# Biased attention on one core: how the last batches of output are closed and who issues their stores

## The chip, the cores and the metric

The kernel runs on one core of a Trainium2 chip. Its engines work side by side: TensorE (PE, with its weight loads shown apart as PEld), VectorE (DVE), ScalarE (ACT), GpSimd (POOL) and SyncE (SP). ScalarE, SyncE and GpSimd can also issue DMAs. In the profile "SPq" and "ACTq" are the instruction queues of SyncE and ScalarE when they issue a DMA or wait. The metric is the device time of one execution in microseconds (us); lower is better. A run's time is a little longer than its profile's span, which goes from the first to the last instruction.

## What is computed

Attention over 4 x 8 = 32 heads, 1024 positions, 64 columns per head, with one bias matrix shared by all heads:

```python
scores = scale * np.matmul(q, k.transpose(0, 1, 3, 2)) + bias
attn = np.exp(scores - scores_max) / (np.sum(np.exp(scores - scores_max), axis=-1, keepdims=True) + 1e-8)
return np.matmul(attn, v)
```

The kernel leaves out the subtraction of the maximum. It gives V a column of ones, so that the sum of the exponentials comes out of the same product as the result, and divides at the end.

## The kernel before

**Slots.** The work is cut into 256 slots. A slot is one head and one of eight chunks of 128 queries; all 1024 keys are done at once. A slot lives in one of three PSUM places (pl0, pl1, pl2), each 128x1024 f32. A slot goes through three steps:

- `fill` (L246, matmuls at L244): TensorE adds q times k for the slot to what its place holds from the slot before. A fill is 8 matmuls, and it must wait until the place's earlier contents have been read.
- `exp` (L253, L258): ScalarE takes the exponential of the place into an SBUF tile `E`. For 19 slots listed in `PLAN`, the last of them slot 243, VectorE does this instead, by a polynomial in six steps (L275, L280, L284, L287, L290, L295), into a tile `de`.
- `av` (L303, matmuls at L312): TensorE multiplies the exponentials by V, 8 matmuls, into 65 columns of a PSUM bank `po`.

**Batches.** Up to seven slots share one `po` bank and make a batch. A batch is closed by `close` (L680), which queues `evac` (L315) on VectorE: a reciprocal of the sums (`rs`, L320) and a multiplication (L322) that writes the finished columns to SBUF. A batch of more than one slot goes to a tile `ob`, of which there are two buffers (L60); a batch of one goes to a tile of its own, `olast` (L74). There are two `po` banks. They are taken in turn by the batches, so that a new batch waits until the batch before the last has been evacuated.

**Stores.** `evac` makes one store to DRAM of each run of neighbouring chunks of one head. A run of one chunk gives 128 rows of 256 bytes (64 columns, 32 KB), of two 64 KB, and of three 96 KB.

**Rounds.** The slots come in rounds. At the end of the kernel a round is three slots of one head, one for each place, with the chunks 0, 1 and 2: slots 247, 248, 249 are a round, then 250 to 252, and 253 to 255. Slot 246 is the last one of the round before. Slot 243 is taken out of the row of its round, since its `de` tile is finished much later.

**Order.** Nothing is reordered on the chip: a planner in the kernel goes through the work with estimated costs and writes out the order in which the instructions of each engine stand. A batch is closed when it has seven slots, or six with no finished `de` tile at hand, or when 255 or 256 slots are done (L638). In `close`, `last` is true for the batches that end with slot 255's neighbour or slot 255: ScalarE issues their stores, all of them, and SyncE those of all other batches (L688). Stores marked `last` stand behind ScalarE's last exponential in its order.

In the order of before, the eleven slots that come last in `av` make three batches:

| batch | slots | stores, issued by |
|---|---|---|
| six slots | 246, 247, 248, 249, 250, 251 | 32 KB, 96 KB, 64 KB by SyncE |
| four slots | 252, 243 (`de`), 253, 254 | 32 KB, 32 KB, 64 KB by ScalarE |
| one slot | 255 | 32 KB by ScalarE |

When all is done, SyncE waits for every store and then all engines go through a closing barrier (shown as L835).

Of the kernel before, what the change touches and what calls it, by code (L numbers as in the profile page):

```python
# [16 lines left out]
def kernel(  # L17
# [13 lines left out]
    nc = tc.nc  # L31
# [59 lines left out]
    round_of = []  # L91
# [19 lines left out]
    NS = len(slots)  # L111
# [191 lines left out]
    def av(group, b, tag):  # L303

        if b not in bank:
            bank[b] = [ps_x.tile([P, 7, D1], F32, tag=tag, name="po"), []]
        po, units = bank[b]
        j = len(units)
        units += group
        for kc in range(NCH):  # L310
            for i, s in enumerate(group):
                nc.tensor.matmul(po[:, j + i, :], etile[s][:, kc, :], vall[:, slots[s][2] % VR, kc, :],  # L312
                                 start=j + i + kc == 0, stop=kc == NCH - 1, skip_group_check=True)

    def evac(b):  # L315

        po, units = bank[b]
        n = len(units)
        rs = small.tile([P, 7, 1], F32, name="rs")
        nc.vector.reciprocal(rs[:, :n, :], po[:, :n, D:D1])  # L320
        ob = olast if n == 1 else op.tile([P, 7, D], F32, name="ob")
        nc.vector.tensor_tensor(ob[:, :n, :], po[:, :n, :D], rs[:, :n, :].to_broadcast([P, n, D]), op=ALU.mult)  # L322
        stores = []

        j = 0
        while j < n:
            x, c, h, start = slots[units[j]]
            i = j + 1
            while i < n and slots[units[i]][1:3] == (c + i - j, h):
                i += 1  # L330
            stores.append((of[:, h, c:c + i - j, :], ob[:, j:i, :]))
            j = i
        return stores

    with tc.manual_schedule():
# [4 lines left out]
        for i in range(2):  # L340
            nc.sync.dma_start(out=k0f[:, :, i * half:(i + 1) * half].rearrange("p t c d -> p t (c d)"),
                              in_=kf[0][:, :, i * half * D:(i + 1) * half * D])
# [52 lines left out]
        L_PE, L_ACT, L_DVE = 205, 210, 140  # L395
# [10 lines left out]
        av_done = {}  # L406
# [21 lines left out]
        dav = []  # L428
# [9 lines left out]
        sp_q, t_sp = [], T0  # L438
# [43 lines left out]
        def next_v(t):  # L482

            while loads_v and not any(x[2] // 2 == loads_v[0] - VR // 2 and y not in av_done for y, x in enumerate(slots)):
                if loads_v[0] - VL not in v_at:
                    break
                p = loads_v.pop(0)
                vland_at[p] = issue(t, 1600, LATE + (p > 12), load_v, p) + 2000
                move_v(p)
# [86 lines left out]
        def pe_cands():  # L576

            out = []
            for x in range(3):
                if not queue[x] or queue[x][0] > next_fill + WINDOW:  # L580
                    continue
                s = queue[x][0]
                r = fill_ready(s)
                if r is not None and (before[s] is None or before[s] in used):
                    cost = FILL + BIAS * bool(slots[s][3] and s > 1)

                    def do(t, s=s, x=x, cost=cost):
                        nonlocal next_fill
                        fill(s)
                        filled[s] = t + cost + L_PE  # L590
                        queue[x].pop(0)
                        next_fill = min([y[0] for y in queue.values() if y], default=NS)
                        if s in PLAN:
                            dslots.add(s)
                            avq.remove(s)
                            start_d(s)
                        else:
                            acts.append(s)
                    out.append((max(t_pe, r), cost, do, 0, s))
# [3 lines left out]
            if avq:  # L603
                group = [s for s in avq[:1] if round_of[s] == round_of[avq[0]]]
                have = [s for s in group if s in e_at]
                lag = len([s for s in avq[:NE] if s in e_at])
                if len(have) < len(group):
                    group = have if lag >= 7 and have[:1] == avq[:1] else []
                if avq[0] >= NS - 3:
                    group = [s for s in avq[:1] if s in e_at]  # L610
# [4 lines left out]
            if todo:  # L615
                r, group = min(todo)
                b = len(closed)
                if b_tag:
                    tag = b_tag[0]
                    group = group[:7 - len(bank[b][1])]  # L620
                else:
                    f, tag = min((x_free[y], y) for y in x_free)
                    r = max(r, f)
                cost = AVG * len(group) if len(group) > 1 else AV
                if r < 1e11:
                    def do(t, group=group, b=b, tag=tag, cost=cost):
                        b_tag[:] = [tag]
                        x_free[tag] = 1e12
                        av(group, b, tag)
                        for s in group:  # L630
                            if s in dslots:
                                dav.pop(0)
                            else:
                                avq.remove(s)
                            av_done[s] = t + cost
                        next_v(t)
                        n = len(bank[b][1])
                        if n == 7 or n == 6 and not (dav and dav[0][0] < t + cost + 600) or len(av_done) in (NS - 1, NS):  # L638
                            closed.append(b)
                            b_tag.clear()  # L640
                            close(b, tag, t + cost + L_PE)
                    out.append((max(t_pe, r), cost, do, 1, 0))
            if pieces:
                pr, which, c0, n = pieces[0]
                need = need_at[pr, which, c0]
                ring = pr + linked(pr) - RING
                lag = len([s for s in avq[:NE] if s in e_at])
                if ((pr, which, c0) in raw_at and next_fill >= need - AHEAD and (ring < 0 or last_slot[ring] < next_fill)
                        and (lag < 4 or need - next_fill < 8)):
                    f, tag = min((x_free[y], y) for y in x_free)  # L650
                    r = max(f, raw_at[pr, which, c0])
                    cost = n * TR + SWITCH * (pr < EARLY or which not in BESIDE)
                    urgent = need - next_fill < 12
                    if r < 1e11:
                        def do(t, pr=pr, which=which, c0=c0, n=n, tag=tag, cost=cost):
                            x_free[tag] = 1e12
                            pieces.pop(0)
                            px = transposes(pr, which, c0, n, tag)
                            if pr < EARLY and which == 0 and c0 == 0:
                                freed(pr, t)  # L660

                            def run(t2):
                                copy_out(pr, which, c0, n, px)
                                done = t2 + 60 * n + (180 if which else 300)
                                x_free[tag] = done + L_DVE
                                if which:
                                    ready["ko", pr] = done + L_DVE
                                else:
                                    ready["qo", pr, c0] = done + L_DVE
                                doubles(pr, which, c0, n, done, urgent)  # L670
                            dve_q.append((t + cost + L_PE, 0 if urgent else 2, 60 * n + (180 if which else 300), run))
                        out.append((max(t_pe, r), cost, do, 2 if next_fill < need - 12 else 0.5, 0))
# [7 lines left out]
        def close(b, tag, t):  # L680
            units = bank[b][1]
            cost = 230 + 120 + 67 * len(units)
            last = len(av_done) >= NS - 1

            def run(t2):
                for to, of_ in evac(b):

                    w = nc.scalar if last else nc.sync  # L688
                    sp_q.append((t2 + cost + L_DVE, lambda t3, to=to, of_=of_: w.dma_start(out=to, in_=of_), last))  # L689
                x_free[tag] = t2 + cost + L_DVE  # L690
            dve_q.append((t, 1, cost, run))

# [76 lines left out]
        while next_fill < NS or next_act < len(acts) or avq or dav or dve_q or sp_q:  # L769
# [15 lines left out]
            stores = [x for x in sp_q if len(x) == 2 or not x[2] or next_act == len(acts)]  # L785
# [6 lines left out]
            t, who = min(c)  # L792
# [47 lines left out]
```

## Time and profile before

| | us |
|---|---|
| three runs | 234.78, 236.41, 235.97 (median 235.97) |
| the profiled execution | 235.12 |
| its span | 233.4 |
| around the span | 1.72 |

The granted TensorE clock of the core is 0.996. ScalarE, TensorE and VectorE are all over 80% busy, and the page's strip of 40 slices shows them so from the fifth slice on:

```profile
## 2 busy tenths in 40 slices
PE   7899998899999999999999999999999999999992
...
DVE  3576777599988998889989789899999899999991
ACT  3699999899999999999999999999999999999992
POOL 8754540276563636304254010000000000000000
```

Each digit is the busy share of 5.8 us, in tenths. Only the last slice is nearly empty: the kernel runs full until some 4 us before its end. GpSimd has been done since the middle.

### The profile page before, as it was taken

The page shows a single profiled execution, that of the slowest core. Times are in us where ns is not written, and L with a number is a line of the kernel's source. Part 1 is how long each engine was busy: PE and PEld are TensorE (multiplying, and loading weights), DVE is VectorE, ACT ScalarE, POOL GpSimd, SP SyncE. Part 2 cuts the span into 40 slices and gives each one's busy share as a digit, 9 for nine tenths or more (in the row PEclk, how much of TensorE's full clock was granted, in tenths as well). Part 3 has the DMA queues.
Part 4 walks back from the last instruction along what each step waited for, and adds up shares of the span by engine and source line. Part 5 has one row for each costly group of instructions (what it writes and reads, how often), then busy time and mean ns, then how long its engine had stood idle before and what let it go on. Part 6 is the DMA issues. An engine that isn't in the chain of part 4 may idle for free.

```text
span 233.4 us, 10661 instructions
## 1 busy us (share of the span) xinstructions
PE 222.4 (95%) x4671; PEld 209.6 (90%) x4671; DVE 197.7 (85%) x290; ACT 221.6 (95%) x242; POOL 61.7 (26%) x99
## 2 busy tenths in 40 slices
PE   7899998899999999999999999999999999999992
PEld 2779997899999999998999999999998999999991
DVE  3576777599988998889989789899999899999991
ACT  3699999899999999999999999999999999999992
POOL 8754540276563636304254010000000000000000
PEclk9999999999999999999999999999999999999998
DMA  6999999899997999989899764111111112112112
GB/s 207 207 206 218 221 226 215 180 112 142 171 173 119 139 188 149 181 188 138 148 234 232 162 108 128 37 37 42 42 40 43 45 42 75 49 31 80 44 37 62
DMA packets 55645, 29.75 MB, mean 127 GB/s; under 512 B 31728, under 2 KB 51952, under 8 KB 55600
## 3 DMA queue, kind: packets, MB, share of 16 engines
q0 software_dynamic: 30336, 14.06, 48.5%
q1 hardware_dynamic: 24544, 14.33, 22.0%
q10 hardware_dynamic: 720, 0.69, 1.1%
q8 instruction: 36, 0.59, 1.1%
q14 instruction: 9, 0.07, 0.1%
HBM read 29.36 MB, written 8.39 MB: 162 GB/s over the span
## 4 chain that ended last, share of the span: by engine, by line
PE 44%; ACT 29%; issue 14%; DVE 5%; DMA 4%; SPq 2%; POOL 1%; DVEq 0%; ACTq 0%; POOLq 0%
ACT E L258 29%; PE pl L244 25%; PE po L312 12%; PE px L191 4%; DMA braw<-in_bias_dram 2%; PE pl L241 2%; SPq L689 2%; DMA out_dram<-ob 1%; DVE ob L322 1%; PE px L187 1%; DVE df L280 1%; DVE dy L275 1%; DVE dt L290 0%; DVE df L287 0%; DVE rs L320 0%
## 5 line engine op out<-in xcount | busy, mean ns | idle before, releaser
L258 ACT ACTIVATE E<-pl 128x1024 bf16<-128x1024 f32 (+1 forms) x238 | 218.4, 1119 | 3.4 <-PE pl L244 3.0
L312 PE MATMUL po<-vall,E 128*128 128x65 bf16 x1896 | 91.9, 194 | 1.7 <-ACT E L258 0.9
L312 PEld LDWEIGHTS <-E 128*128 128x128 bf16 x1896 | 77.4, 98 | 2.8 <-ACT E L258 1.2
L244 PE MATMUL pl<-qo,ko 128*128 128x128 bf16 x1024 | 76.9, 219 | 1.1 <-ACT E L258 0.6
L244 PEld LDWEIGHTS <-ko 128*128 128x128 bf16 x1160 | 69.4, 98 | 3.9 <-issue 0.9
L244 PE MATMUL pl<-qe,ke 128*128 128x128 bf16 x888 | 66.2, 219 | 2.1 <-issue 0.7
L244 PEld LDWEIGHTS <-ke 128*128 128x128 bf16 x888 | 53.4, 98 | 4.9 <-issue 1.3
L275 DVE TENSOR_SCALAR dy<-pl 128x1024 int32<-128x1024 f32 x19 | 23.2, 1221 | 4.4 <-PE pl L244 3.6
L322 DVE TENSOR_TENSOR ob<-po,rs 128x448 f32<-128x448 f32 (+2 forms) x39 | 23.2, 594 | 2.3 <-DVE rs L320 0.4
L284 DVE SCALAR_TENSOR_TENSOR dt<-df 128x1024 f32<-128x1024 f32 x19 | 23.2, 1220 | 0.3
L295 DVE SCALAR_TENSOR_TENSOR de<-dy,dt 128x1024 uint16<-128x1024 int32 x19 | 23.2, 1219 | 0.2
L287 DVE SCALAR_TENSOR_TENSOR df<-dt,df 128x1024 f32<-128x1024 f32 x19 | 23.1, 1220 | 0.1
L290 DVE SCALAR_TENSOR_TENSOR dt<-df,dt 128x1024 f32<-128x1024 f32 x19 | 23.1, 1219 | 0.1
L138 POOL DMA_DIRECT2D q<-in_q_dram x18 | 16.4, 911 | 7.0 <-DVE rs L320 5.4
L165 POOL DMA_DIRECT2D v<-in_v_dram x16 | 11.3, 705 | 20.9 <-DVE rs L320 9.9
L199 DVE COPY ko<-px 128x1024 bf16<-128x1024 bf16 (+1 forms) x16 | 10.8, 672 | 6.6 <-PE px L191 6.2
L201 DVE TENSOR_SCALAR qo<-px,sgn 128x1024 bf16<-128x1024 bf16 (+2 forms) x18 | 12.4, 686 | 4.2 <-PE px L191 2.6
L320 DVE RECIPROCAL rs<-po 128x7 f32<-128x7 f32 (+3 forms) x40 | 7.9, 197 | 7.2 <-PE po L312 7.0
L280 DVE TENSOR_SCALAR df<-dy 128x1024 f32<-128x1024 uint16 x19 | 13.3, 700 | 0.1
L241 PE MATMUL pl<-ident,braw 128*128 128x128 bf16 x136 | 11.6, 229 | 0.4 <-DMA braw<-in_bias_dram 0.3
L145 POOL DMA_DIRECT2D k<-in_k_dram x15 | 10.7, 713 | 2.2 <-DMA k<-in_k_dram 1.2
L241 PEld LDWEIGHTS <-braw 128*128 128x128 bf16 x136 | 9.9, 149 | 0.7 <-DMA braw<-in_bias_dram 0.5
(54 smaller groups left out, 119.9 us busy)
## 6 DMA issues: line engine op xcount, KB each, us to landing
v<-in_v_dram POOLq DMA_DIRECT2D x16, 256.0 KB, 6.1
k<-in_k_dram POOLq DMA_DIRECT2D x15, 256.0 KB, 6.3
out_dram<-ob SPq DMA_DIRECT2D x34, 96.0 KB, 3.6
ke<-ko SPq DMA_DIRECT2D x22, 128.0 KB, 4.7
out_dram<-ob SPq DMA_DIRECT2D x41, 64.0 KB, 2.3
q<-in_q_dram POOLq DMA_DIRECT2D x18, 128.0 KB, 4.9
qe<-q SPq DMA_DIRECT2D x17, 128.0 KB, 4.4
out_dram<-ob SPq DMA_DIRECT2D x67, 32.0 KB, 2.8
```

Of the source, the lines that this page charges most:

```text
L138: nc.gpsimd.dma_start(out=t[:, :, y, :], in_=(qf, kf)[x][pr][:, y].rearrange("p (c d) -> p c d", d=D))
L241: nc.tensor.matmul(to, braw[:, c, :].rearrange("p (kp kc) -> p kc kp", kc=NCH)[:, kc, :], ident8[:], start=i == 0, stop=False, skip_group_ ...
L244: nc.tensor.matmul(to, kk[:, kc, :], qq[:, c, :], start=False, stop=True, skip_group_check=True)
L258: nc.scalar.activation(e[:, i:i + n].rearrange("p b x -> p (b x)"), places[slots[s][0]][:, i:i + n].rearrange("p b x -> p (b x)"), ACTF.Ex ...
L275: w.tensor_scalar(t["y"][:], places[slots[s][0]].rearrange("p b x -> p (b x)"), scale * LOG2E * 65536.0, 127.0 * 65536.0, op0=ALU.mult, op ...
L280: w.tensor_scalar(t["f"][:], t["lo"], G / 65536.0, None, op0=ALU.mult)
L284: w.scalar_tensor_tensor(t["t"][:], t["f"][:], -G, t["f"][:], op0=ALU.add, op1=ALU.mult)
L287: w.scalar_tensor_tensor(t["f"][:], t["t"][:], Q, t["f"][:], op0=ALU.mult, op1=ALU.add)
L290: w.scalar_tensor_tensor(t["t"][:], t["f"][:], V, t["t"][:], op0=ALU.add, op1=ALU.mult)
L295: w.scalar_tensor_tensor(etile[s].bitcast(U16).rearrange("p c q -> p (c q)"), t["y"][:], 1.0 / 512.0, t["t"][:], op0=ALU.mult, op1=ALU.add)
L312: nc.tensor.matmul(po[:, j + i, :], etile[s][:, kc, :], vall[:, slots[s][2] % VR, kc, :], start=j + i + kc == 0, stop=kc == NCH - 1, skip_ ...
L322: nc.vector.tensor_tensor(ob[:, :n, :], po[:, :n, :D], rs[:, :n, :].to_broadcast([P, n, D]), op=ALU.mult)
```

## The change

```diff
                         n = len(bank[b][1])
-                        if n == 7 or n == 6 and not (dav and dav[0][0] < t + cost + 600) or len(av_done) in (NS - 1, NS):
+
+                        z = group[-1]
+                        if (n == 7 or n == 6 and not (dav and dav[0][0] < t + cost + 600) or len(av_done) == NS
+                                or z >= NS - 2 or z >= NS - 10 and round_of[z] != round_of[z + 1]):
                             closed.append(b)
@@ in close
             def run(t2):
-                for to, of_ in evac(b):
-
-                    w = nc.scalar if last else nc.sync
-                    sp_q.append((t2 + cost + L_DVE, lambda t3, to=to, of_=of_: w.dma_start(out=to, in_=of_), last))
+                stores = evac(b)
+                for i, (to, of_) in enumerate(stores):
+
+                    end = last and i == len(stores) - 1
+                    w = nc.scalar if end else nc.sync
+                    sp_q.append((t2 + cost + L_DVE, lambda t3, to=to, of_=of_, w=w: w.dma_start(out=to, in_=of_), end))
```

The first part closes a batch after slot 246 and from there on wherever a round ends, and after slots 254 and 255. The second part leaves to ScalarE only the last store of each of the last two batches and gives the others to SyncE. The eleven slots now make five batches:

| batch | slots | stores, issued by |
|---|---|---|
| one slot (`olast`) | 246 | 32 KB by SyncE |
| three slots | 247, 248, 249 | 96 KB by SyncE |
| three slots | 250, 251, 252 | 96 KB by SyncE |
| three slots | 253, 243 (`de`), 254 | 32 KB (253) and 32 KB (243) by SyncE, 32 KB (254) by ScalarE |
| one slot (`olast`) | 255 | 32 KB by ScalarE |

Slot 243 now stands between 253 and 254 in its batch, so that the chunks of 253 and 254 are no longer neighbours and go out in two stores.

On the engines: TensorE has the same matmuls, in another order over the last 240 rows of its order. VectorE has two reciprocals and two multiplications more (five pairs for the three of before), and the first two extra pairs stand ahead of steps L287 and L295 of slot 243. ScalarE issues two stores where it issued four; SyncE issues five where it issued three. All instructions ahead of that, some 222 us of the profiled execution, are the same on every engine.

## The prediction

> **What bounds the kernel now.** I read the page first, for the engine that is full; then the stretch from 222 us on in order of time for ScalarE, VectorE and TensorE, since nothing ahead of it changes; then the DMA view of the last microseconds and SyncE's waits, for what ends the run.
>
> The page's totals, and ScalarE from 222 us (start, length, engine, line, operation, count):
>
> ```profile
> PE 222.4 (95%) x4671; PEld 209.6 (90%) x4671; DVE 197.7 (85%) x290; ACT 221.6 (95%) x242; POOL 61.7 (26%) x99
> ```
> ```profile
> 221.62 7.57 ACT L258 ACTIVATE E<-pl 128x1024 bf16<-128x1024 f32 x8
> 229.47 1.31 ACTq L689 DMA_DIRECT2D out_dram<-ob  x3
> 230.88 0.39 ACTq L689 DMA_DIRECT2D out_dram<-olast  x1
> ```
>
> ScalarE runs eight exponentials without a gap. One lasts about 1.15 us and the next starts 0.92 us after it (7.57 less 1.15, over 7), so they end at 222.75, 223.67, 224.60, 225.52, 226.43, 227.35, 228.27 and 229.19. Then it issues three stores back to back until 230.78, and only then that of `olast`. VectorE in the same stretch:
>
> ```profile
> 222.52 0.19 DVE L320 RECIPROCAL rs<-po 128x6 f32<-128x6 f32 x1
> 222.74 0.56 DVE L322 TENSOR_TENSOR ob<-po,rs 128x384 f32<-128x384 f32 x1
> 223.22 1.21 DVE L287 SCALAR_TENSOR_TENSOR df<-dt,df 128x1024 f32<-128x1024 f32 x1
> 224.47 1.23 DVE L290 SCALAR_TENSOR_TENSOR dt<-df,dt 128x1024 f32<-128x1024 f32 x1
> 225.73 1.23 DVE L295 SCALAR_TENSOR_TENSOR de<-dy,dt 128x1024 uint16<-128x1024 int32 x1
> 226.87 0.19 DVE L320 RECIPROCAL rs<-po 128x6 f32<-128x6 f32 x1
> 227.09 0.56 DVE L322 TENSOR_TENSOR ob<-po,rs 128x384 f32<-128x384 f32 x1
> 228.80 0.18 DVE L320 RECIPROCAL rs<-po 128x4 f32<-128x4 f32 x1 [1.15 <-PE po L312]
> 229.01 0.42 DVE L322 TENSOR_TENSOR ob<-po,rs 128x256 f32<-128x256 f32 x1
> 229.71 0.17 DVE L320 RECIPROCAL rs<-po 128x1 f32<-128x1 f32 x1 [0.28 <-PE po L312]
> 229.91 0.23 DVE L322 TENSOR_TENSOR olast<-po,rs 128x64 f32<-128x64 f32 x1
> ```
>
> `olast` is complete at 230.14, and its store starts at 230.88: 0.74 us in which the last result waits for ScalarE's queue. `ob` ended at 229.43 and its store began at 229.47, so a store needs only 0.04 us after its data. Then the landing, from the DMA view of 228 us on (KB each, us from issue to landing), the row of the page for large stores, and SyncE's last wait:
>
> ```profile
> out_dram<-ob SPq DMA_DIRECT2D x1, 96.0 KB, 1.7
> out_dram<-olast ACTq DMA_DIRECT2D x1, 32.0 KB, 1.5
> ```
> ```profile
> out_dram<-ob SPq DMA_DIRECT2D x34, 96.0 KB, 3.6
> ```
> ```profile
> SPq L835 <- DMA out_dram<-olast: 0.4, 1, 0.4
> ```
>
> The store of `olast` lands at 230.88 + 1.5 = 232.38, it is the last thing waited for, and 1.0 us of closing barrier brings the span to 233.4. So the path of the end is: last exponential 229.19, its product (229.24 to 229.67), the `olast` pair (to 230.14), 0.74 us of queue, 1.5 us of landing, 1.0 us of barrier.
>
> **ScalarE's two stores fewer.** The three stores ahead of `olast` (0.35 + 0.44 + 0.44, with gaps 1.31 us) become one of 0.35 us. It can start when `ob` of the batch of 253, 243, 254 is written. That batch's last product is slot 254's, as before, so its reciprocal starts at 228.80 again; the multiplication has 192 columns, which by the rows of 64 (0.23) and 256 columns (0.42) takes 0.36 us: 229.01 to 229.37. ScalarE's store then runs from 229.41 to 229.76, and ScalarE is free when `olast` is complete at 230.14. The store of `olast` starts at 230.18 where it was 230.88: **minus 0.70 us**.
>
> **SyncE's two stores more.** They start at 229.41 and about 229.76 (0.35 us, then 0.43 us). SyncE was free from 228.95 on in before; here the 96 KB store of slots 250 to 252 comes just ahead, from 228.42 to about 228.85. The second of the two lands at 229.76 + 1.55 = 231.31, ahead of `olast` at 230.18 + 1.5 = 231.68. Cost nothing; if an issue took 1.18 us, as one of SyncE's at 223.7 did, the second would start at 230.59 and land at 232.14, and 0.46 of the 0.70 would be lost.
>
> **Four small stores close together.** Before, one of them had 512-byte rows; now all four have 256-byte rows, since 243 splits 253 from 254. This strip is 231.2 to 232.2 in 40 slices, each digit the busy share of the 16 DMA engines:
>
> ```profile
> DMA  0000559899986421000000034899774210000000
> ```
>
> The first burst is the 64 KB store, 0.35 us; the second is `olast`, 32 KB, 0.30 us, 0.87 us after its issue. The two 32 KB bursts ahead of them took 0.28 us. Stacked one after the other from 229.41 + 0.87 = 230.28, four bursts of 0.28 end at 231.40; `olast` alone would end at 230.18 + 0.87 + 0.28 = 231.33. So contention costs nothing to 0.07 us; I take 0.06, as two are issued at the same moment. The Trainium skill ("DMA: Bandwidth & Descriptors", Specifications) says that a transfer needs at least 512 B for line rate, since below this the DMA engine reads, modifies and writes; this speaks against the split. The trace agrees that half the bytes are hardly cheaper. By the rule taken whole, 32 KB in short rows would be as dear as 64 KB in long ones, which leaves an estimated gain of 0.35; rival 1 works this out from rows.
>
> **VectorE's two pairs more.** A pair of 64 columns takes 0.43 us (229.71 to 230.14), one of 192 columns 0.57. Before L287 comes the pair of slot 246: L287 moves from 223.22 to 223.63, L290 ends at 226.11. Then the pair of 247 to 249, whose last product (slot 249) is there by 225.5: to 226.64. L295 then ends at 227.87, where it ended at 226.96. Its `de` is wanted by slot 243's product, which now stands behind that of 253 (exponential done 227.35, product started by 227.68), so TensorE waits for `de` until 227.9 and is done issuing it by 228.19, ahead of slot 254 at 228.33. The pair of 250 to 252 fills 227.87 to 228.42, ahead of 228.80. Cost nothing, under this cover: `de` may be 0.14 us later before slot 254's product moves, and another 0.34 before its pair runs into the `olast` pair at 229.71. Beyond 0.48 us every bit shows.
>
> **TensorE's order.** Two bank changes more, each with a wait for an evacuation. Slot 247 waits for the bank that VectorE frees at 223.30 (the pair at 222.52 above). Ahead of it stands a fill that was behind it, released by the exponential that ended at 222.75:
>
> ```profile
> 222.42 0.68 PE L312 MATMUL po<-vall,E 128*128 128x65 bf16 x16
> 222.93 0.61 PE L244 MATMUL pl<-qe,ke 128*128 128x128 bf16 x8
> 224.66 0.61 PE L244 MATMUL pl<-qe,ke 128*128 128x128 bf16 x8 [0.31 <-ACT E L258]
> 229.24 0.43 PE L312 MATMUL po<-vall,E 128*128 128x65 bf16 x8 [0.48 <-ACT E L258]
> ```
>
> With it the fill runs from about 222.8 to 223.25 and the wait is 0.1 us. The later banks are free at 223.65, 226.64 and 228.42, ahead of their use at 225.4, 227.4 and 229.24. TensorE must be ready for the fill at 224.66, since the exponential at 225.3 follows it directly; from 223.33 it has 0.26 + 0.45 + 0.26 us of issuing for that (eight `av` matmuls take half of the first row's 0.52, eight fills 0.45), so 0.36 us are left. Cost nothing; past that, ScalarE stalls by the excess.
>
> **Sum.** -0.70 + 0.06 = -0.64 us: the span 233.4 becomes 232.76, the profiled time 235.12 becomes 234.48. That execution lies 0.85 below the median; the median, 235.97, becomes 235.33. What is late next is the landing and the barrier, which stay.
>
> **Rivals.**
> 1. *A part of the gain* (0 to 0.5 us): the SyncE issue of 1.18 us, the stacked bursts, or `de` late. If VectorE's extra 0.41 + 0.50 us ahead of L295 cost twice that, 0.43 of it passes the cover and the gain is 0.21: 235.8. If a 32 KB burst among others takes the 0.35 us of the 64 KB one, the four end at 231.68 and the gain is 0.35: 235.6; I give this 0.05 of the rival's chance, as both lone 32 KB bursts ahead took 0.28. For the long issue: one took 1.18. Against: the other eleven after 214 us took 0.33 to 0.43.
> 2. *The second `ob` buffer decides, and it gets slower.* The `ob` of 253, 243, 254 reuses the buffer of slots 247 to 249, whose 96 KB store is issued only at 226.68. If that lands later than 229.0 (2.3 us after its issue) the pair waits; past 229.34 (2.7 us) `olast` stands behind it on VectorE; past 3.4 us the whole gain is gone. With the page's 3.6 us it lands at 230.28, the pair ends at 230.64, `olast` at 231.07 and its store starts at 231.11: 0.23 later than before, 236.2. For: 3.6 is the median of all 34. Against: that was with loads on the DMA engines; the row of the last microseconds has 1.7.
> 3. *More than forecast*: the fill at 222.93 moves ahead by 0.13 us, and if ScalarE turned out to follow TensorE there, that would come on top: gain 0.8, 235.2. ScalarE has no gap, so little speaks for it.
>
> That the change does not reach the chip's order is no case here: the order of stores and pairs is written out.
>
> **Chances and range.** Forecast 0.70, rival 1 0.17, rival 2 0.08, rival 3 0.05. All cases lie within 1% (2.36 us, about what a measurement can tell from no change), so faster or slower by over 1% could come only from the scatter of runs, 234.78 to 236.41 in before: 0.03 each. The range takes the lowest of those less 0.70, 234.1, up to the highest with nothing gained, 236.4.
>
> **What would show it.** Right: `olast`'s store issued within 0.1 us of its multiplication, the last exponential still ending near 229.2, no gap on ScalarE from 222 us on, L295 about 0.9 us later with TensorE waiting for `de` and not for slot 254's place, the span near 232.8. Wrong: a gap on ScalarE at 225.3, VectorE waiting for a store ahead of the 192-column multiplication at 229.0, or SyncE's last wait on a store of `ob` instead of `olast`.

## The result and the profile after

| | before | after |
|---|---|---|
| median, first comparison | 235.42 us (8 runs) | 234.21 us (8 runs) |
| ratio, 95% interval | | 0.9948 [0.9922, 0.9973] |
| profiled execution | 235.12 us | 234.37 us |
| its span | 233.4 us | 232.6 us |
| last exponential ends | 229.19 us | 229.16 us |
| from there to the end of the span | 4.2 us | 3.4 us |

The kernel became about half a percent faster in this comparison, and 0.4% faster in two later ones (below). The two profiled executions differ by 0.75 us and their spans by 0.80, of which 0.77 lies behind the last exponential. This stretch, from the end of the last exponential to the end of the span, is called the tail below. The pages of the profile round the span to 0.1 us; the traces end at 233.355 and 232.557, so the tails are 4.17 and 3.40 us. The tails below are reckoned from such ends, while the expectations were written with rounded spans (3.44 for after). The tail can be compared between profiles, since it leaves out the first 229 us, whose length changes from run to run by more than the gain: in the traces of this case the last exponential ends anywhere from 228.54 to 229.48 us.

ScalarE after, in order of time (start, length, engine, line, operation, count):

```profile
217.97 11.19 ACT L258 ACTIVATE E<-pl 128x1024 bf16<-128x1024 f32 x12
229.38 0.36 ACTq L694 DMA_DIRECT2D out_dram<-ob  x1
230.15 0.34 ACTq L694 DMA_DIRECT2D out_dram<-olast  x1
```

The twelve exponentials are one unbroken stretch. One store stands ahead of `olast`'s where three stood, and ScalarE is idle from 229.74 until the last result is there. VectorE after:

```profile
223.19 0.16 DVE L320 RECIPROCAL rs<-po 128x1 f32<-128x1 f32 x1
223.38 0.22 DVE L322 TENSOR_TENSOR olast<-po,rs 128x64 f32<-128x64 f32 x1
223.53 1.21 DVE L287 SCALAR_TENSOR_TENSOR df<-dt,df 128x1024 f32<-128x1024 f32 x1
224.77 1.23 DVE L290 SCALAR_TENSOR_TENSOR dt<-df,dt 128x1024 f32<-128x1024 f32 x1
225.91 0.17 DVE L320 RECIPROCAL rs<-po 128x3 f32<-128x3 f32 x1
226.12 0.36 DVE L322 TENSOR_TENSOR ob<-po,rs 128x192 f32<-128x192 f32 x1
226.40 1.22 DVE L295 SCALAR_TENSOR_TENSOR de<-dy,dt 128x1024 uint16<-128x1024 int32 x1
...
228.99 0.36 DVE L322 TENSOR_TENSOR ob<-po,rs 128x192 f32<-128x192 f32 x1
229.69 0.17 DVE L320 RECIPROCAL rs<-po 128x1 f32<-128x1 f32 x1 [0.34 <-PE po L312]
229.89 0.23 DVE L322 TENSOR_TENSOR olast<-po,rs 128x64 f32<-128x64 f32 x1
```

The last multiplication ends at 230.12 and its store starts at 230.15. Before, the two were 0.74 us apart. The extra pairs stand ahead of L287 and L295; L295 ends at 227.62. TensorE after, some of its rows:

```profile
222.80 0.61 PE L244 MATMUL pl<-qe,ke 128*128 128x128 bf16 x8
223.33 0.43 PE L312 MATMUL po<-vall,E 128*128 128x65 bf16 x8
224.63 0.61 PE L244 MATMUL pl<-qe,ke 128*128 128x128 bf16 x8
227.67 0.43 PE L312 MATMUL po<-vall,de 128*128 128x65 bf16 x8
229.22 0.43 PE L312 MATMUL po<-vall,E 128*128 128x65 bf16 x8 [0.48 <-ACT E L258]
```

The fill that was at 222.93 stands ahead of the product at 223.33, the fill that ScalarE follows is at 224.63 where it was at 224.66, and slot 243's product (`de`) starts at 227.67, 0.05 us after its tile is complete and well ahead of slot 254's, which starts at 228.30. TensorE hardly waits for the tile: slot 253's product keeps it issuing until about 227.65. SyncE's last two stores (the row spans both), the landings of the last stores, and SyncE's last waits:

```profile
229.37 0.81 SPq L694 DMA_DIRECT2D out_dram<-ob  x2
```
```profile
out_dram<-ob SPq DMA_DIRECT2D x2, 32.0 KB, 1.5
out_dram<-ob ACTq DMA_DIRECT2D x1, 32.0 KB, 1.7
out_dram<-olast ACTq DMA_DIRECT2D x1, 32.0 KB, 1.5
```
```profile
SPq L840 <- DMA out_dram<-ob: 0.7, 2, 0.5
SPq L840 <- DMA out_dram<-olast: 0.3, 1, 0.3
```

`olast` is still the last store to land, 1.5 us after its issue. By the trace, the 0.77 us of the tail are 0.71 us by which its store starts earlier, 0.05 by which it lands sooner after that (1.51 to 1.45), and 0.01 behind the landing. The issue itself became 0.05 us shorter, too: it took 0.39 us directly behind three other stores and takes 0.34 on an idle queue.

### The profile page after: what moved, and what is told of

It is laid out like the page before. It is cut to its first block, busy times and chain, and to the rows that moved or that the text cites. A ratio compares the mean times of both kernels' runs of the same rounds, so it can differ in the third digit from the quotient of the medians.

```text
span 232.6 us, 10671 instructions
## 1 busy us (share of the span) xinstructions
PE 223.1 (96%) x4671; PEld 209.8 (90%) x4671; DVE 197.4 (85%) x294; ACT 221.6 (95%) x242; POOL 61.6 (27%) x99
## 4 chain that ended last, share of the span: by engine, by line
PE 42%; ACT 30%; issue 14%; DMA 5%; DVE 4%; POOL 3%; SPq 2%; DVEq 0%; ACTq 0%; POOLq 0%
ACT E L258 30%; PE pl L244 24%; PE po L312 12%; DMA q<-in_q_dram 4%; PE px L191 4%; SPq L694 2%; PE pl L241 2%; DVE ob L322 1%; DMA out_dram<-ob 1%; DVE dy L275 1%; POOL k L145 1%; DVE df L280 1%; POOL braw L160 1%; DVE dt L290 0%; DVE de L295 0%
## 5 line engine op out<-in xcount | busy, mean ns | idle before, releaser
L295 DVE SCALAR_TENSOR_TENSOR de<-dy,dt 128x1024 uint16<-128x1024 int32 x19 | 23.1, 1218 | 0.1
L287 DVE SCALAR_TENSOR_TENSOR df<-dt,df 128x1024 f32<-128x1024 f32 x19 | 23.1, 1218 | 0.1
L468 POOL COPY tick<-q 1x1 bf16<-1x1 bf16 x9 | 3.3, 365 | 28.4 <-DMA q<-in_q_dram 28.4
```

The source lines that it names most:

```text
L287: w.scalar_tensor_tensor(t["f"][:], t["t"][:], Q, t["f"][:], op0=ALU.mult, op1=ALU.add)
L295: w.scalar_tensor_tensor(etile[s].bitcast(U16).rearrange("p c q -> p (c q)"), t["y"][:], 1.0 / 512.0, t["t"][:], op0=ALU.mult, op1=ALU.add)
```

## The experiments

The theory was: the gain is the time that the last result waited in ScalarE's queue, so it belongs to the second part of the change. The rivals: it belongs to the closing by rounds; or a part of the measured 1.2 us comes from somewhere else. In the diffs, three dots stand for further lines.

**The second part alone.** The kernel before, with the new `close` and the old condition for closing.

```diff
-                for to, of_ in evac(b):
-                    w = nc.scalar if last else nc.sync
+                stores = evac(b)
+                for i, (to, of_) in enumerate(stores):
+                    end = last and i == len(stores) - 1
+                    w = nc.scalar if end else nc.sync
...
```

> Only the second part of the change: the batches close as before, ScalarE issues the last store of each of the last two. Measured by the tail, from the end of the last exponential to the end of the span: 4.2 us in before, 3.44 in after. Theory (the whole gain is the wait of the last result behind ScalarE's stores): ScalarE issues one 64 KB store at 229.47 and the olast store at 230.18; tail 3.4 to 3.5, the time within 0.3 us of after. Rival (closing by rounds carries the gain): tail near 4.2, time as before.

Median 234.57 us, ratio 0.9973 [0.9947, 0.9998]. The last exponential ends at 229.16, the span at 232.6: a tail of 3.42 us, for 3.40 in after. ScalarE in this kernel:

```profile
223.40 5.76 ACT L258 ACTIVATE E<-pl 128x1024 bf16<-128x1024 f32 x6
229.44 0.37 ACTq L691 DMA_DIRECT2D out_dram<-ob  x1
230.14 0.34 ACTq L691 DMA_DIRECT2D out_dram<-olast  x1
```

`olast`'s store starts 0.98 us after the last exponential, as in after (0.99), with the old three batches. So the second part alone gives 0.75 of the 0.77 us. The time was expected within 0.3 us of after, and this was missed: measured beside it, after has 234.18 (below), 0.39 less. The twelve runs of this kernel spread from 233.33 to 235.65, and the profiles leave no place for 0.39 us: from the start of the eighth last exponential to the end of the last one it is 7.56 us in both kernels, and ahead of that their instructions are the same. So it is taken for scatter.

**The first part alone.** The changed kernel with the old `close`.

```diff
-                stores = evac(b)
-                for i, (to, of_) in enumerate(stores):
-                    end = last and i == len(stores) - 1
-                    w = nc.scalar if end else nc.sync
...
+                for to, of_ in evac(b):
+                    w = nc.scalar if last else nc.sync
...
```

> Only the first part of the change: batches close with their rounds, and ScalarE issues all four stores of the last two batches. Theory: three stores of 32 KB from 229.41 to about 230.68 stand ahead of olast, whose store starts at about 230.78 instead of 230.88; tail 4.1, gain 0.1 us at most. Rival (closing by rounds carries the gain): tail 3.5 to 3.7.

Median 234.80 us, ratio 0.9987 [0.9967, 1.0007]; the tail is 4.09 us (229.46 to 233.54), where 4.1 was expected. ScalarE:

```profile
223.70 5.76 ACT L258 ACTIVATE E<-pl 128x1024 bf16<-128x1024 f32 x6
229.67 1.31 ACTq L692 DMA_DIRECT2D out_dram<-ob  x3
231.08 0.39 ACTq L692 DMA_DIRECT2D out_dram<-olast  x1
```

Here `olast`'s store starts 1.62 us after the last exponential, against 1.69 in before: 0.07 us, because the multiplication has 192 columns for 256 (0.36 for 0.42 us). This is all that the closing by rounds brings by itself, and beside the second part it brings next to nothing (a tail of 3.40 us for 3.42).

**Another way out of the queue.** The kernel before, with nothing changed but the engine that issues the store of `olast`.

```diff
-                    w = nc.scalar if last else nc.sync
...
+                    end = last and len(stores) > 1
+                    w = nc.scalar if end else nc.sync
...
```

> Before, with one store moved: ScalarE keeps the three stores of the batch of four, SyncE issues that of olast. Theory: SyncE is free, olast is issued at 230.18 and lands at 231.7, but ScalarE's third store, 64 KB, issued at 230.34, lands at 231.94 and now ends the run: tail 3.75, gain 0.45 us, and SyncE's last long wait is on ob. Rival (SyncE starts a store later than ScalarE does, or the order of SyncE's waits matters): tail 4.0 or more.

The tail is 3.77 us (228.84 to 232.61), where 3.75 was expected; the median is 234.44 us, and the ratio 0.9990 [0.9964, 1.0016] doesn't tell this from no change. ScalarE's three stores and SyncE's one:

```profile
229.12 1.31 ACTq L690 DMA_DIRECT2D out_dram<-ob  x3
```
```profile
229.82 0.33 SPq L690 DMA_DIRECT2D out_dram<-olast  x1
```

`olast` starts 0.98 us after the last exponential from SyncE too and lands in 1.5 us, so it doesn't matter here which of the two engines issues it, only that nothing is queued ahead. ScalarE's third store, the 64 KB one, is now the last: issued at 229.99, it lands 2.80 us after the last exponential, where `olast` lands 2.44 us after it in after. The Trainium skill ("DMA: Bandwidth & Descriptors", Issuing engines are not separate DMA queues) says that issuing from several engines saves only the sequencer's time to start a DMA, usually small beside the DMA itself. The traces agree: a landing still takes 1.5 to 1.7 us, an issue 0.33 to 0.44. But three issues in a row ahead of the last result are 1.31 us, and at the end of a program nothing hides them.

**Is the rest scatter?** The tails differ by 0.77 us; the first medians by 1.21. The changed kernel was run again, and a third time beside the halves (below).

> The changed kernel once more, beside new runs of before. The tails of the two profiles differ by 0.77 us, the medians by 1.2. If the rest is scatter of the runs of before (which lie in two clusters, 234.6 to 234.9 and 235.9 to 236.4): the difference here is nearer to 0.77, or the runs of the other kernels of this call, whose first 222 us are the same, show the upper cluster too. If it belongs to the change: the difference is 1.2 again and no run of this kernel is above 235.

> After, in the same call as the halves, so that both share the runs of before. Expected ratio about 0.9967 (tail shorter by 0.77 us of 235); the median within 0.3 us of the halves.

| | before | after | ratio |
|---|---|---|---|
| first | 235.42 (8 runs) | 234.21 (8) | 0.9948 [0.9922, 0.9973] |
| second | 234.97 (35) | 234.18 (12) | 0.9964 [0.9943, 0.9984] |
| third | 234.93 (23) | 234.19 (12) | 0.9957 [0.9939, 0.9976] |

After gives 234.2 each time; it is before that moves. With 35 and 23 runs of before the medians differ by 0.79 and 0.74, which fits the tail. The two clusters of the first eight runs of before are not there in the 35, which fill the gap between them, and the other kernels measured beside them go up to 235.5 and beyond too. The tail itself repeats: it is 3.40, 3.39 and 3.40 us in the three profiles of after (of before there is one). All three intervals hold 0.9967 (0.77 of 235), though all three ratios lie below it. So a further tenth of a percent can't be excluded, but the profiles show no place for it: the last eight exponentials take 7.56 to 7.57 us in before and in all three of after, and ahead of them every engine has the same instructions in the same order.

**The output buffer.** The three batches of three slots share one buffer, in a tile that is dead by then.

```diff
-        ob = olast if n == 1 else op.tile([P, 7, D], F32, name="ob")
+        ob = olast if n == 1 else qz[0].bitcast(F32).rearrange("p c x -> p (c x)")[:, :3 * D].rearrange("p (c d) -> p c d", d=D) if n == 3 else op.tile([P, 7, D], F32, name="ob")
```

> After, with the three batches of three slots sharing one output buffer, so that each of their multiplications waits for the store of the one ahead; nothing is changed before 222 us but the place of these tiles. It doses the wait for an output buffer that the prediction priced as the way to a slower kernel. Tail of after: 3.4 us. Theory (a store lands about 1.65 us after its issue here): the batch of 250 to 252 waits until about 228.15 on the clock of the profile of after and its store is issued at 228.6, the batch of 253, 243, 254 waits until about 230.25, olast stands behind it on VectorE and its store starts at about 231.1 instead of 230.15; tail 4.2 to 4.5, as long as before or longer. Rival (the wait is hidden because the final product is later anyway): tail 3.4 to 3.7.

A single time: 235.48 us, beside 235.06 of before on the same chip; the tail is 4.84 us (228.85 to 233.69), longer than in before. Single times scatter by more than this difference; the tail is what is read here. VectorE:

```profile
227.99 0.36 DVE L322 TENSOR_TENSOR qz<-po,rs 128x192 f32<-128x192 f32 x1 [0.59 <-DMA out_dram<-qz]
228.46 0.18 DVE L320 RECIPROCAL rs<-po 128x3 f32<-128x3 f32 x1
230.08 0.36 DVE L322 TENSOR_TENSOR qz<-po,rs 128x192 f32<-128x192 f32 x1 [1.43 <-DMA out_dram<-qz]
230.35 0.16 DVE L320 RECIPROCAL rs<-po 128x1 f32<-128x1 f32 x1
230.54 0.22 DVE L322 TENSOR_TENSOR olast<-po,rs 128x64 f32<-128x64 f32 x1
```

The mechanism of the prediction's second rival is real: two waits for landings, 2.0 us in all, and `olast` behind them on VectorE. `olast` is ready 1.91 us after the last exponential; the expectation had its store start at 1.94, and it starts at 2.11. The tail came out longer than the 4.2 to 4.5 expected, since the stores now come together: `olast`'s is issued 0.2 us after its data, behind ScalarE's other store, and lands 1.7 us after its issue instead of 1.5. With two buffers VectorE waits for no store in this stretch.

**The cover of `de`.** One more VectorE step of 1.2 us, which computes nothing that is used, ahead of slot 243's last step.

```diff
         def last():
+            if s == PLAN[-1]:
+                x = braw[:, :2].bitcast(F32).rearrange("p c k -> p (c k)")
+                w.scalar_tensor_tensor(x, x, 1.0, x, op0=ALU.add, op1=ALU.mult)
```

> After, with one more VectorE step of the size of the polynomial's (128x1024 f32 in a tile that is no longer used, 1.2 us) just ahead of the last step of slot 243. It doses the cover of the de tile. In after L295 ended at 227.62 where 227.87 was reckoned, so the cover is 0.48 + 0.25 = 0.73 us. Theory: of the 1.13 to 1.2 us that the step adds, some 0.4 shows at the end: tail 3.8, VectorE without idle time before the last two batches. Rival (the cover is much larger, or de does not reach the path): tail 3.4 to 3.5. Other rival (no cover): tail 4.6.

A single time: 234.85 us, beside 235.06 of before. TensorE, then ScalarE, then the landing of `olast`:

```profile
228.53 0.43 PE L315 MATMUL po<-vall,de 128*128 128x65 bf16 x8 [1.00 <-DVE de L298]
228.81 0.72 PE L315 MATMUL po<-vall,E 128*128 128x65 bf16 x16
```
```profile
229.87 0.36 ACTq L697 DMA_DIRECT2D out_dram<-ob  x1
230.33 0.39 ACTq L697 DMA_DIRECT2D out_dram<-olast  x1
```
```profile
out_dram<-olast ACTq DMA_DIRECT2D x1, 32.0 KB, 1.7
```

TensorE waits a full microsecond for `de`, and the products of 254 and 255 run together behind it. `olast` is complete 1.28 us after the last exponential for 0.96 in after: of the 1.13 us that the step adds (L298 starts that much after it), 0.32 passes the cover (the time that `de` may be late without any effect on the end), so the cover was about 0.8 us, where 0.73 was reckoned. The tail is 4.17 us, more than the 3.8 expected: `olast`'s store again finds ScalarE's other store just ahead (0.16 us from data to issue, 0.03 in after), lands in 1.69 us for 1.45, and from there to the end of the span it is 1.03 us for 0.96.

**A shorter end.** The exponential of slot 255 in two halves.

```diff
-                exp(s)
+                if s == NS - 1:
+                    exp(s, 0, 1)
+                    exp(s, 1, 1)
+                else:
+                    exp(s)
```

> After, with the exponential of slot 255 in two halves of 512 columns, so that TensorE can do the first four of its eight products while ScalarE is at the second half. An attempt at a shorter end than that of after. On the tail counted from the end of the last exponential: four products less, 0.45 to about 0.32 us, tail 3.3. On the time: if a half costs ScalarE exactly half of the 0.92 us spacing, 0.13 us less; if a second instruction costs 0.1 us or more of its own, nothing is won or up to 0.1 lost.

> The kernel with the last exponential in halves, timed. Its profile had a tail of 3.29 us after the last exponential, 0.15 less than after, while the last five slots took ScalarE 0.09 us longer: net 0.05 to 0.06 us ahead of after. Expected against before: a ratio of about 0.996 (0.83 us of 235), as for after within what can be measured; its single time of 233.67 should prove to be scatter of the first 222 us. Other reading (the halves win more than the profile shows): ratio below 0.993.

The tail is 3.30 and 3.29 us in the two profiles, and `olast`'s store starts 0.85 us after the last exponential instead of 0.99. But the two halves take ScalarE more than one whole exponential. The last six slots in the timed kernel, and in after:

```profile
223.65 5.82 ACT L258 ACTIVATE E<-pl 128x1024 bf16<-128x1024 f32 x7
```
```profile
223.41 5.75 ACT L258 ACTIVATE E<-pl 128x1024 bf16<-128x1024 f32 x6
```

That is 0.07 us more (the 0.09 of the expectation was reckoned from a spacing, and is replaced by this), and leaves 0.03 to 0.04 of the 0.10 to 0.11 us that the tail is shorter. The first single time, 233.67 us, was scatter: twelve runs have a median of 234.04 and a ratio of 0.9968 [0.9939, 0.9996], and after, measured beside them, has 0.9957. A few hundredths of a microsecond can't be measured in the times, so this is not shown to beat after.

## Why the prediction was right, point by point

- **The queue.** Predicted: `olast`'s store 0.70 us earlier. Measured in the profiles, from the last exponential: 1.69 to 0.99 us, 0.70. The second part alone shows the same, the first part alone 0.07. The signs named for this came true: the store starts 0.03 us after its data, the last exponential ends at 229.16, ScalarE has no gap, and SyncE's last wait on a store is for `olast`.
- **SyncE's two stores.** Predicted from 229.41 and 229.76; they ran from 229.37 for 0.81 us and landed in 1.5. The issue of 1.18 us did not come back there; one of 1.26 us stands at 224.16, far from the end. (Of the others after 214 us, twelve and not eleven took 0.33 to 0.43.)
- **The bursts.** Predicted at 0.06 us of loss, which did not appear: `olast` landed in 1.5 us. The term stood for stores stacked one after the other, and they are not stacked: by the trace the packets of SyncE's store run from 230.21 to 230.47 and those of ScalarE's, issued at the same moment, from 230.32 to 230.59, side by side and each as long as one store alone (0.27 us). The cost fell on a store that nobody waited for: of the two, ScalarE's landed in 1.7. When `olast` itself comes that close to others (0.08 us behind a store of SyncE's with the extra step, 0.11 with the one buffer), it is `olast` that takes 1.7. This kernel stays clear of that by the 0.4 us between the last store of `ob` and that of `olast`. A price of 0.35 us for each 32 KB burst, which would have left 0.35 us of gain, did not show: they took 0.27, and the 64 KB one in before 0.34.
- **VectorE.** L295 was put at 227.87 and ended at 227.62. The term was too dear: the pairs moved L287 by 0.31 us and L295 by another 0.36, instead of 0.41 and 0.50, since an instruction that needs nothing of the one ahead starts up to 0.08 us before that one's end (0.36 + 226.12 = 226.48, and L295 starts at 226.40). (By its own figures the prediction's first evacuation of three ends at 226.11 + 0.57 = 226.68 and not at 226.64; it ended at 226.48.) The cover was reckoned from the later time and so came out as 0.48 us; it is about 0.8. So one sign did not come true: L295 was to end about 0.9 us later with TensorE waiting for `de`, and it ended 0.66 later, with no wait to speak of.
- **TensorE.** The wait at slot 247 was put at 0.1 us; the product starts at 223.33, 0.05 after VectorE's pair ended at 223.28, and the fill at 224.63 is not late. Slot 246's result goes to the tile `olast` too, so that slot 255's multiplication may write it only when slot 246's store is done. The prediction did not price this; the store was issued at 225.99, behind others in SyncE's queue, and landed by 227.5, 2.4 us ahead of the multiplication at 229.89.
- **The sum.** A gain of 0.64 us, against 0.77 in the tail, 0.75 between the profiled executions and 0.74 to 1.21 between medians. Most of the difference from the tail is the 0.06 of the bursts, which was not lost, and the 0.05 of the landing, which was not reckoned. The time of 235.33 us missed the 234.21 measured by 1.12 us, more than the gain itself, because the median it was taken from was too high: 235.97 of three runs, where larger sets give 234.9 to 235.4. That the measured time still lies in the range, 0.1 us above its lower end, is owed to the lowest of those three runs, and is luck; that the gain is right is not.
- **Rivals.** By the prediction's times the second buffer decides only if a 96 KB store takes 2.7 us or more; it was issued at 226.50 and took 1.6. The third rival's gain of 0.8 us is near what was measured, but its mechanism did not act: the last eight exponentials take 7.56 us, as in before.

## What to carry to other kernels

At the end of a program the last result should find the queue of the engine that issues its store empty: put the stores that come shortly before it on another engine, and let the last of them start well ahead. Here 0.33 to 0.39 us ahead was enough (`olast` landed in 1.45 to 1.48 us) and 0.08 to 0.11 was not (1.69 to 1.70); for `olast` nothing between was measured. (Where SyncE issued `olast`, ScalarE's 64 KB store followed it by 0.17 us and landed in 1.64, as in before.) Of the two parts of this change, the one that moves the stores is what pays. Work that is added to an engine off the path is free only under a cover that can be reckoned from the trace, and it pays to check the cover by adding to it. To tell a gain of 0.7 us in 235, compare the stretch of the profile that the change touches, from a mark that lies ahead of it.

## What was not expected of the hardware

Two stores of 32 KB issued in the same moment, one from each engine, land after 1.45 us (SyncE's) and 1.66 us (ScalarE's), and a third, issued by SyncE 0.38 us behind them, after 1.55. A lone one of ScalarE's took 1.50 in before. The busy share of the DMA engines after, 230 to 232 us in 40 slices of 0.05 us:

```profile
DMA  0000479997300169831049951000000000000000
```

The first hump is the two together, 0.39 us from the first packet to the last; the second is SyncE's next store and the third `olast`, 0.27 us each, with gaps between them. So the two overlap. ScalarE's, issued last by 4 ns, starts to move 0.12 us later than SyncE's and lands 0.45 us after its last packet, where SyncE's lands after 0.35: a store that collides lost 0.16 to 0.24 us in the traces here, partly ahead of its packets and partly behind them. Why is not shown.
